# Moving the last thirteen modulation dot products of a two-layer encoder kernel to an earlier place in the program

## The chip, the cores and the metric

The kernel runs on one core of a Trainium2 chip. Its engines are TensorE (PE, whose weight loads are listed as PEld), VectorE (DVE), ScalarE (ACT), GpSimd (POOL) and SyncE (SP), whose queue issues the DMA transfers. The metric is the device time of one execution in microseconds; a kernel's time is the median of several runs.

## The reference

The reference is a trunk of two layers over one sequence of 1024 tokens with 1024 features. Layer 0 mixes tokens by differential attention (eight heads, each with two softmax maps of 64 features, whose difference weighs 128 value features), layer 1 by multi-head latent attention. Each layer first normalises its input and applies a shift and a scale that depend on a conditioning vector `c`, and at its end adds its output times a gate that depends on `c` too:

```
def _modulation(c, ada_w, ada_b):
    mod = jax.nn.silu(c) @ ada_w + ada_b
    shift, scale, gate = jnp.split(mod[:, None, :], 3, axis=-1)
    return shift, scale, gate

for i in range(DEPTH):
    shift, scale, gate = _modulation(c, ada_w[i], ada_b[i])
    h = _rmsnorm(x, norm_g[i]) * (1.0 + scale) + shift
    y = _diff_attention(h, ...) if i % N_MIXERS == 0 else _mla(h, ...)
    x = x + gate * y
return _rmsnorm(x, final_norm_g)
```

In the differential attention, `q`, `k`, `v` and a gate `z` come from one projection of `h`; queries and keys are rotated by position (rope); `p = softmax(map 0) - lam * softmax(map 1)`; the output is `p @ v`, normalised per head, times `silu(z)`, and projected by `w_out`.

## The kernel before, in words

**Precision and tiles.** A product of two float32 matrices is computed as three matmuls of rounded halves (`mm3`, high by high, high by low, low by high; lines 203 to 205). A strip is a 128-column piece of a projection for all 1024 tokens, in two halves of 512 tokens; a half takes eight steps of three matmuls. A value tile is 128 tokens by the 512 value columns of four heads, again eight steps, 24 matmuls (`v0_tile`). Value tiles are written to DRAM and read back later head by head.

**The place of the change.** The values of heads 0 to 3 are done. Then come, for head 0, the second half of the key strip, the second half of the query strip, and the gate strip (`stream0.step(Z_PRE)`, sixteen steps, both halves). After them the eight value tiles of heads 4 to 7 are computed, `tt` from 0 to 7. Ahead of tile 6 (`V_LATE`) the PSUM banks are handed out anew and the first query tile of the attention is emitted: its scores (L905), row maxima `nm` (L433), exponentials `e` (L436) and their combination (L911 to L913). The stream of strips goes on with the key strip of head 1 (`acc` with the matmuls L203 to L205).

**An eviction of a value tile** (`store_v`) is a cast on ScalarE and a subtraction on VectorE, both at L393, into a buffer `v_hl`, and a store of 512 KB into `vS` on the SP queue (L395). Tiles 0 to 5 share two buffers in the pool `p1b`, tiles 6 and 7 take theirs from the pool `pm` under the name of the dots' buffers. There are five accumulator banks up to tile 5, and two after it.

**The modulation.** `gen_mods` yields 24 dot products of 128 x 1024: sixteen for the shifts and scales of layer 1, eight for the gate of layer 0. Each one is a load of a 512 KB piece of the weights (L455, SP queue, name `ada`), and a multiply-and-sum on VectorE with a read of its accumulator (L476). Their results are needed only later: the gate column is written out (L492) for the end of layer 0, and layer 1 comes after that. Seven dots are emitted before the place of the change, two in the key half and two in the query half; from the latter's end on, their buffers are three in the pool `pm`:

```
    mod_home[0] = lambda src: mod_load(src, pm, 3)
```

The other thirteen are emitted in the loop over the value tiles, `MODS[tt]` ahead of tile `tt`.

**What sets the order.** The text gives what is emitted; a scheduler with its own costs then orders the instructions of each engine by their dependencies, so that order on an engine is not the order of the text. `tc.issue_after` and `tc.keep_in_program_order` constrain it. The rope of the first key and query strips is queued in `side` as small steps; `pend` holds those that are left, and the first four are emitted before the gate strip, two more ahead of each tile from tile 2 on. On POOL stand the rope's multiplications and subtractions (L355, L370, L377, L378) and the low halves of the strip weights (L254). The transfers L384 swap the two halves of the partitions of `qa` and `qb`. The loads L931 are weights for the query strip of head 1, issued after tile 5 (`HOLD`).

Of the kernel before, what the change touches and what calls it, by code (L numbers as in the profile page):

```python
# [44 lines left out]
SPL1 = 2  # L45
Z_PRE = 16
V_LATE = 6
MODS = (2, 2, 2, 2, 3, 2, 0, 0)
QA_V = 16
V_IN = 4  # L50
V1_AT = ((2, 4), (3, 4), (0, 6), (0, 6))
# [47 lines left out]
def trunk(ctx: ExitStack, tc: tile.TileContext, A, out):  # L99
# [186 lines left out]
    def gen_strips(items, w=None):  # L286


        w = w or split_strip(items[0][0]())
        raws = items[1][0]()  # L290
        for i, (_, rhs, consume) in enumerate(items):
            nxt = ([], [])
            at = [0, 5][: len(raws)]
            for half in range(2):
                for k, _ in enumerate(gen_half(w, rhs, half, lambda acc, half=half, consume=consume: consume(acc, half))):
                    if half == 1 and k in at:
                        for a, b in zip(nxt, split_raw(*raws.pop(0))):
                            a += b
                        if not raws and i + 2 < len(items):
                            raws = items[i + 2][0]()  # L300
                            at = at[: at.index(k) + 1]
                    yield
            w = nxt
# [191 lines left out]
    def gen_mods(load, c2):  # L495

        g, bsh, bsc, a_, b_ = mods[1]
        for j in range(KT):
            for i, (bias, acc) in enumerate(((bsh, b_), (bsc, a_))):
                mod_dot(load(A["ada_ss1"][j, i]), bias[:, j : j + 1], acc[:, j : j + 1], c2)  # L500
                if j == KT - 1 and i == 1:
                    V.scalar_tensor_tensor(out=a_, in0=a_, scalar=1.0, in1=g, op0=ALU.add, op1=ALU.mult)
                yield
        yield from gen_gate(0, load, c2)
# [178 lines left out]
    mods_g = gen_mods(lambda src: mod_home[0](src), c2)  # L683
# [192 lines left out]
    stream0 = Stream(gen_strips(items[2:], wz0))  # L876
# [13 lines left out]
    for t in pend[:4]:  # L890
        t()
    turn = 0
    stream0.step(Z_PRE)

    def q_tile(h, half, ti, zz, ep, mid=lambda i: None):

        ql = slice(ti * P, (ti + 1) * P)
        zs = [zz[:, ti : ti + 1], sm.tile([P, 1], F32, name="z1")]
        es = []
        qa, qb = QS[h][half]  # L900
        for c in range(2):
            s_ps = bank("sc", "s", [P, T])
            for src, fst in ((qa, True), (qb, False)):
                for kc in range(2):
                    PE.matmul(s_ps[:, kc * HF : (kc + 1) * HF], src[:, c, ql], KS[h][kc][:, c, :], start=fst, stop=not fst)  # L905
            with tc.issue_after(combined[-1]) if c == 0 and combined else nullcontext():
                es.append(softmax_part(None if c else ep, s_ps, zs[c], 1 if ep is a0a else 3))
            mid(c)
        e0, e1 = es
        z0, z1 = zs  # L910
        V.reciprocal(z1, z1)  # L911
        V.tensor_scalar(z1, z1, z0, neglam[:, 0:1], op0=ALU.mult, op1=ALU.mult)
        combined.append(V.scalar_tensor_tensor(out=e0, in0=e1, scalar=z1[:, 0:1], in1=e0, op0=ALU.mult, op1=ALU.add).ins)  # L913
        return e0

    first, combined = [], []
    for tt in range(8):
        if tt == V_LATE:
            psum("ps2", sc=2, tr=1, pv=1)
            zz0 = sm.tile([P, 4], F32, name="zz")  # L920
            first += [zz0, q_tile(0, 0, 0, zz0, a0a)]
        for _ in range(MODS[tt]):
            next(mods_g)
# [1220 lines left out]
```

## Time and profile before

| | us |
|---|---|
| median of three runs | 1419.05 |
| the three runs | 1411.88, 1419.73, 1419.05 |
| the profiled execution, its time | 1413.83 |
| its span | 1412.0 |
| TensorE busy in it | 1374.9 |
| VectorE busy | 936.7 |
| ScalarE busy | 740.3 |
| GpSimd busy | 610.6 |

The mean granted clock of TensorE is 0.995 of full speed. In the rows of single instructions the columns are the start in us from the span's start, the duration in us, the engine, the line of the kernel, the operation, output <- inputs, and in brackets the idle time of the engine before it with what ended it. Rows of groups have a count, then the busy time and the mean of one in ns, then the idle time before. Busy times of engines overlap; only TensorE's are near to the span.

### The profile page before, as it was taken

Reading aid. Unit: us, or ns where it says so; the run is one execution under the profiler, and the core shown is the slowest. Engines: PE = TensorE matmul, PEld = TensorE weight load, DVE = VectorE, ACT = ScalarE, POOL = GpSimd, SP = SyncE. Lnnn points to the kernel's source line nnn. Section 1 sums busy time; section 2 is a strip of 40 time slices with the busy share of each in tenths; the row PEclk is TensorE's granted clock in tenths of the full one; section 3 lists DMA queues with packets and bytes.
Section 4 is the critical chain, followed back from the end, with each engine's and each line's share of the span. In section 5 each row is a group of like instructions: output and inputs, shape, how many; then the busy total and the mean of one; then the engine's idle time right before and its main releaser. Section 6 shows DMA issues by size and latency. Waiting matters only on the chain.

```text
span 1412.0 us, 20440 instructions
## 1 busy us (share of the span) xinstructions
PE 1374.9 (97%) x7254; PEld 1150.0 (81%) x7254; DVE 936.7 (66%) x1365; ACT 740.3 (52%) x1290; POOL 610.6 (43%) x484
## 2 busy tenths in 40 slices
PE   9999899999999999999999999999999999998997
PEld 7778688888888888787778878888888888887886
DVE  7756687676777767678445787346777776764455
ACT  6623366666565655566443654345555555644342
POOL 4415164646564646462563235513142432313662
PEclk9999999999999999999999999999999999999999
DMA  9877723233333232336672222448688787776663
GB/s 352 262 226 233 237 66 103 79 103 83 105 85 95 80 96 81 97 87 221 219 240 97 97 90 90 126 146 261 164 223 248 213 240 195 204 214 214 226 213 129
DMA packets 147736, 230.98 MB, mean 164 GB/s; under 512 B 19121, under 2 KB 70449, under 8 KB 147634
## 3 DMA queue, kind: packets, MB, share of 16 engines
q1 hardware_dynamic: 147634, 229.68, 53.5%
q8 instruction: 57, 0.93, 0.3%
q14 instruction: 45, 0.37, 0.1%
HBM read 145.79 MB, written 60.23 MB: 146 GB/s over the span
## 4 chain that ended last, share of the span: by engine, by line
PE 78%; DMA 7%; DVE 6%; issue 3%; ACT 3%; SPq 2%; POOL 1%; ACTq 0%; POOLq 0%; DVEq 0%
PE acc L203 9%; PE acc L205 9%; PE acc L204 9%; PE s L1831 8%; PE s L905 7%; PE tr L414 6%; PE pv L204 4%; PE pv L205 4%; PE pv L203 4%; PE oacc L204 3%; PE oacc L205 3%; PE oacc L203 3%; PE zacc L203 1%; PE zacc L205 1%; PE zacc L204 1%
## 5 line engine op out<-in xcount | busy, mean ns | idle before, releaser
L433 DVE TENSOR_REDUCE nm<-s 128x1 f32<-128x1024 f32 x192 | 234.0, 1219 | 87.8 <-PE s L905 66.6
L416 ACT CAST pth<-tr 128x512 fp32r<-128x512 f32 x200 | 117.4, 587 | 212.8 <-PE tr L414 211.9
L436 ACT ACTIVATE e<-s,nm 128x1024 f32<-128x1024 f32 x128 | 143.2, 1119 | 94.6 <-DVE nm L433 94.2
L419 DVE TENSOR_TENSOR ptl<-tr,pth 128x512 fp32r<-128x512 f32 x200 | 137.2, 686 | 75.8 <-ACT pth L416 75.7
L254 POOL TENSOR_TENSOR wl<-wraw,wh 128x512 fp32r<-128x512 f32 (+2 forms) x82 | 102.7, 1254 | 170.4 <-ACT wh L253 162.8
L203 PE MATMUL acc<-h0h,wh 128*128 128x512 f32 x360 | 151.6, 421 | 1.8 <-DVE v_hl L393 1.7
L203 PE MATMUL pv<-pth,vt 128*128 128x256 f32 x512 | 146.4, 286 | 0.0
L204 PE MATMUL pv<-ptl,vt 128*128 128x256 f32 x512 | 145.2, 284 | 0.1
L205 PE MATMUL pv<-pth,vt 128*128 128x256 f32 x512 | 144.5, 282 | 0.0
L205 PE MATMUL acc<-h0h,wl 128*128 128x512 f32 x360 | 143.3, 398 | 0.1
L204 PE MATMUL acc<-h0l,wh 128*128 128x512 f32 x360 | 142.4, 396 | 0.0
L414 PE MATMUL tr<-ident,e 128*128 128x128 f32 x800 | 120.9, 273 | 10.1 <-DVE ptl L419 10.0
L414 PEld LDWEIGHTS tr<-ident,e 128*128 128x128 f32 x800 | 96.2, 140 | 41.6 <-DVE ptl L419 16.3
L1234 POOL TENSOR_TENSOR wol<-wor,woh 128x512 fp32r<-128x512 f32 x64 | 86.6, 1372 | 77.4 <-ACT woh L1233 71.4
L204 PEld LDWEIGHTS pv<-ptl,vt 128*128 128x128 f32 x512 | 97.2, 190 | 5.1 <-DVE ptl L419 0.4
L203 PEld LDWEIGHTS pv<-pth,vt 128*128 128x128 f32 x512 | 97.0, 189 | 4.5 <-ACT pth L416 0.4
L205 PEld LDWEIGHTS pv<-pth,vt 128*128 128x128 f32 x512 | 97.6, 191 | 0.1
L905 PE MATMUL s<-ks,qa 128*128 128x512 f32 x256 | 82.7, 403 | 6.0 <-ACT e L436 3.0
L913 DVE SCALAR_TENSOR_TENSOR e<-s,z,e 128x1024 f32<-128x1024 f32 x64 | 82.1, 1283 | 2.1
L355 POOL TENSOR_TENSOR rp_sw<-rp_sw,sinT 128x512 f32<-128x512 f32 x42 | 55.3, 1316 | 62.8 <-DMA rp_sw<-rp_raw 57.6
L205 PEld LDWEIGHTS acc<-h0h,wl 128*128 128x128 f32 x360 | 68.3, 190 | 16.4 <-POOL wl L254 0.6
L905 PE MATMUL s<-ks,qb 128*128 128x512 f32 x256 | 81.1, 396 | 0.0
(632 smaller groups left out, 3442.2 us busy)
## 6 DMA issues: line engine op xcount, KB each, us to landing
ada<-in_ada_ss SPq DMA_DIRECT2D x32, 512.0 KB, 6.4
wraw<-in_w_s SPq DMA_DIRECT2D x64, 256.0 KB, 2.8
vS<-v_hl SPq DMA_DIRECT2D x32, 512.0 KB, 5.0
vt<-vS SPq DMA_DIRECT2D x32, 512.0 KB, 5.0
wor<-in_w_out SPq DMA_DIRECT2D x64, 256.0 KB, 4.2
pS<-eT SPq DMA_DIRECT2D x28, 512.0 KB, 2.9
pr<-pS SPq DMA_DIRECT2D x56, 256.0 KB, 6.2
rp_sw<-rp_raw SPq DMA_DIRECT2D x168, 64.0 KB, 2.0
```

Of the source, the lines that this page charges most:

```text
L203: pin(PE.matmul(psum, ah, bh, start=first, stop=False))
L204: pin(PE.matmul(psum, ah, bl, start=False, stop=False))
L205: mm = PE.matmul(psum, al, bh, start=False, stop=last)
L254: sub = (lo_on or (V if pair_of else G)).tensor_sub(l_[:, :n], raw[:, :n], f32v(h_[:, :n]))
L414: pin(PE.transpose(tr[:, j, :], p[:, kt * P : (kt + 1) * P], ident))
L416: cp = S.copy(pth[kh][:, :, dst], tr)
L419: mk["V"] = V.tensor_sub(ptl[kh][:, :, dst], tr, f32v(pth[kh][:, :, dst])).ins
L433: mk["V"] = V.reduce_max(nm, s_ps, axis=AX.X, negate=True).ins
L436: ex = S.activation(e, s_ps, AF.Exp, bias=nm, scale=1.0, accum_out=zs)
L905: PE.matmul(s_ps[:, kc * HF : (kc + 1) * HF], src[:, c, ql], KS[h][kc][:, c, :], start=fst, stop=not fst)
L1234: in_turn(G.tensor_sub(lo, raw, f32v(hi)))
L1831: pin(PE.matmul(s_ps[:, kc * HF : (kc + 1) * HF], lhs, rhs(kc), start=i == 0, stop=i == 4))
```

## The change

Before, the thirteen dots are emitted 2, 2, 2, 2, 3, 2 ahead of value tiles 0 to 5. After it, three are emitted ahead of the first gate strip, two between its halves, and two ahead of each of tiles 0 to 3.

```diff
 V_LATE = 6
-MODS = (2, 2, 2, 2, 3, 2, 0, 0)
+MODS = (2, 2, 2, 2, 0, 0, 0, 0)
+MODS_Z = (3, 2)
 ...
     turn = 0
-    stream0.step(Z_PRE)
+    for n in MODS_Z:
+        for _ in range(n):
+            next(mods_g)
+        stream0.step(Z_PRE // len(MODS_Z))
```

Lines behind the second place move by up to four, lines before it by one. Computation, buffers and transfers are otherwise the same.

The first place is VectorE up to the eviction of value tile 3. Before, the last rows of that stretch read as follows; `v_hl_1291` is the eviction of tile 2, `v_hl_1338` that of tile 3, and each `ada` row is a dot, with the read of its accumulator under it.

```order
L476 ISA ada_1176,moda1_92<-ada_1176,c2_228,vec_88 128x1024
L476 ISA moda1_92 128x1
L476 ISA ada_1179,modb1_93<-ada_1179,c2_228,vec_88 128x1024
L476 ISA modb1_93 128x1
L393 TENSOR_TENSOR v_hl_1291<-vps_1266,v_hl_1291 128x512
L476 ISA ada_1211,moda1_92<-ada_1211,c2_228,vec_88 128x1024
L476 ISA moda1_92 128x1
L476 ISA ada_1214,modb1_93<-ada_1214,c2_228,vec_88 128x1024
L476 ISA modb1_93 128x1
L393 TENSOR_TENSOR v_hl_1338<-vps_1313,v_hl_1338 128x512
```

These four are dots 12 to 15 of the 24. In the changed kernel the same stretch reads so; `v_hl_1306` is tile 2 and `v_hl_1354` tile 3, and the dots of `ada_1104`, `ada_1107`, `ada_1110`, `ada_1146` and `ada_1149` (12 to 16) stand above the rows shown.

```order
L477 ISA ada_1193,gcol_1192<-ada_1193,c2_228,vec_88 128x1024
L477 ISA gcol_1192 128x1
L477 ISA ada_1196,gcol_1192<-ada_1196,c2_228,vec_88 128x1024
L477 ISA gcol_1192 128x1
L394 TENSOR_TENSOR v_hl_1306<-vps_1281,v_hl_1306 128x512
L477 ISA ada_1228,gcol_1192<-ada_1228,c2_228,vec_88 128x1024
L477 ISA gcol_1192 128x1
L477 ISA ada_1231,gcol_1192<-ada_1231,c2_228,vec_88 128x1024
L477 ISA gcol_1192 128x1
L394 TENSOR_TENSOR v_hl_1354<-vps_1329,v_hl_1354 128x512
```

Nine dots, 12 to 20, stand ahead of the eviction of tile 3, where there were four. Of the remaining four, two come before the evictions of tiles 6 and 4, in this order, and two before those of tiles 7 and 5; the first row maximum follows behind them, with no dot after it.

The second place is the SP queue, from the first dot load there. Before, `v_hl_1207` is the store of tile 0 and `v_hl_1242` that of tile 1:

```order
L230 DMA wraw_1104<-in_w_s0 128x512
L230 DMA wraw_1106<-in_w_s0 128x512
L455 DMA ada_1176<-in_ada_ss1 128x1024
L455 DMA ada_1179<-in_ada_ss1 128x1024
L395 DMA vS0_1_70<-v_hl_1207 256x4x128
L455 DMA ada_1211<-in_ada_ss1 128x1024
L455 DMA ada_1214<-in_ada_ss1 128x1024
L395 DMA vS0_1_70<-v_hl_1242 256x4x128
```

In the changed kernel `v_hl_1224` is the store of tile 0 and `v_hl_1259` that of tile 1:

```order
L456 DMA ada_1107<-in_ada_ss1 128x1024
L456 DMA ada_1110<-in_ada_ss1 128x1024
L231 DMA wraw_1113<-in_w_s0 128x512
L231 DMA wraw_1115<-in_w_s0 128x512
L456 DMA ada_1146<-in_ada_ss1 128x1024
L456 DMA ada_1149<-in_ada_ss1 128x1024
L456 DMA ada_1193<-in_ada_g0 128x1024
L456 DMA ada_1196<-in_ada_g0 128x1024
L396 DMA vS0_1_70<-v_hl_1224 256x4x128
L456 DMA ada_1228<-in_ada_g0 128x1024
L456 DMA ada_1231<-in_ada_g0 128x1024
L396 DMA vS0_1_70<-v_hl_1259 256x4x128
```

The store of tile 1 stands behind the loads of nine dots (12 to 20, that of `ada_1104` just above the rows shown) where it stood behind four. With three buffers, the load of a dot waits for the dot three before it. The cast of tile 3 on ScalarE waits for the store of tile 1, since both use the same of the two buffers.

The third place is TensorE behind the value tiles. Before, the end of value tile 7 (`vps_1473`), the third score tile and the beginning of the key strip of head 1 (`acc_1517`):

```order
L203 MATMUL vps_1473<-wvh_943,h0h7_1_132 128x512
L204 MATMUL vps_1473<-wvl_944,h0h7_1_132 128x512
L205 MATMUL vps_1473<-wvh_943,h0l7_1_133 128x512
L905 MATMUL s_1508<-ks_1091,qa_1255 128x512
L905 MATMUL s_1508<-ks_1098,qa_1255 128x512
L905 MATMUL s_1508<-ks_1091,qb_1256 128x512
L905 MATMUL s_1508<-ks_1098,qb_1256 128x512
L203 MATMUL acc_1517<-h0h0_0_102,wh_1141 128x512
```

After the change, the first score tile (`s_1424`) stands inside the strip:

```order
L206 MATMUL acc_1517<-h0h3_0_114,wl_1158 128x512
L204 MATMUL acc_1517<-h0h4_0_118,wh_1176 128x512
L205 MATMUL acc_1517<-h0l4_0_119,wh_1176 128x512
L909 MATMUL s_1424<-ks_1091,qa_1270 128x512
L909 MATMUL s_1424<-ks_1098,qa_1270 128x512
L909 MATMUL s_1424<-ks_1091,qb_1271 128x512
L909 MATMUL s_1424<-ks_1098,qb_1271 128x512
```

The first two score tiles stood within tile 7 and the third ahead of the strip; now the first two stand behind 14 matmuls of the strip. Before, tile 7 had a PSUM bank of its own beside that of tile 6, and the strip took the bank of tile 6; now tile 7 takes the bank of tile 6, and the strip the other. In both, the first matmul of tile 6 waits for the eviction of tile 3. On every engine the two orders coincide again in the attention of the first heads.

## The prediction

> **What bounds the kernel now.** I read the page first, then the stretches between 150 and 170 us, then single instructions of each engine between 120 and 163 us, because the change touches only dot products that run there.
>
> ```profile
> span 1412.0 us, 20440 instructions
> PE 1374.9 (97%) x7254; PEld 1150.0 (81%) x7254; DVE 936.7 (66%) x1365; ACT 740.3 (52%) x1290; POOL 610.6 (43%) x484
> ```
>
> TensorE is busy for 97% of the span. So whatever the change does can only be paid in TensorE idle time or in a lower granted clock, and little is left to win: 37 us in the whole span. The next view cuts out the end of the second half's value tiles. The columns are busy time of PE, PEld, DVE, ACT and POOL, the granted clock, the DMA share and GB/s.
>
> ```profile
> 150.00:155.00 5.00, 1.81 (x7) 0.86 (x5) 5.00 (x8) 1.40 (x3) 0.00 (x0) 1.00 0.91 260
> 155.00:160.00 5.00, 3.44 (x8) 2.76 (x9) 4.12 (x8) 2.18 (x4) 0.00 (x0) 0.59 0.89 288
> 160.00:165.00 5.00, 5.00 (x18) 3.91 (x18) 3.07 (x4) 0.00 (x0) 0.00 (x0) 0.73 0.65 200
> 165.00:170.00 5.00, 5.00 (x24) 3.88 (x23) 1.92 (x4) 3.26 (x6) 1.29 (x1) 1.00 0.24 59
> ```
>
> Here TensorE stands still for 4.8 us while VectorE is full, and then runs at a lowered clock. The single instructions say why: first TensorE, then VectorE and one of ScalarE.
>
> ```profile
> 121.00 0.50 PE L203 MATMUL vps<-wvh,h0h 128*128 128x512 f32 x1 [0.37 <-DVE gz L842]
> 137.49 0.39 PE L203 MATMUL vps<-wvh,h0h 128*128 128x512 f32 x1
> 153.66 0.73 PE L905 MATMUL s<-ks,qa 128*128 128x512 f32 x2 [3.04 <-ACT e L436]
> 156.56 0.80 PE L203 MATMUL acc<-h0h,wh 128*128 128x512 f32 x1 [1.72 <-DVE v_hl L393]
> 162.28 0.59 PE L204 MATMUL acc<-h0l,wh 128*128 128x512 f32 x1
> ```
>
> ```profile
> 149.94 1.28 DVE L476 CUSTOM_DVE_ANT_0 ada<-ada,c,vec 128x1024 f32<-128x1024 f32 x1
> 151.15 1.22 DVE L433 TENSOR_REDUCE nm<-s 128x1 f32<-128x1024 f32 x1
> 152.28 1.27 DVE L476 CUSTOM_DVE_ANT_0 ada<-ada,c,vec 128x1024 f32<-128x1024 f32 x1
> 153.49 1.28 DVE L476 CUSTOM_DVE_ANT_0 ada<-ada,c,vec 128x1024 f32<-128x1024 f32 x1
> 154.69 1.22 DVE L433 TENSOR_REDUCE nm<-s 128x1 f32<-128x1024 f32 x1
> 155.83 0.68 DVE L393 TENSOR_TENSOR v_hl<-vps,v_hl 128x512 fp32r<-128x512 f32 x1
> 152.40 1.11 ACT L436 ACTIVATE e<-s,nm 128x1024 f32<-128x1024 f32 x1 [3.18 <-DVE nm L433]
> ```
>
> The late dots (L476) stand between the first row maxima (nm) and the last value evictions (v_hl). The third score tile waits for the first exponential, which waited for nm behind a dot; the next strip waits for v_hl behind two dots and the second nm.
>
> I number the 24 dots in their order; the change moves 12 to 24. I number the eight value tiles of the second half of heads 0 to 7. Each tile is 24 matmuls.
>
> **Term 1, what goes: the loss around 150 to 163 us.** Idle is 3.04 + 1.72 = 4.76 us. Three tiles, 72 matmuls, lie between the starts at 121.00 and 137.49, so a step is 16.49 / 72 = 0.229 us. From 156.56 to 162.70 stand 14 matmuls, counted up to the row that follows the quoted one at 162.28; they took about 0.43 us each, 6.14 us, where 14 × 0.227 = 3.18 us were enough. The slow clock cost 2.96 us. With the dots gone from there, all of it goes: **−7.7 us**.
>
> **What the change puts in its place.** Five dots now stand before or within the first gate strip, and two before each of tiles 0 to 3. On VectorE nine dots come ahead of the eviction of tile 3, not four. This matters twice. Every dot needs a 512 KB load in one of three buffers, so the load three dots on waits for it, on the SP queue, in which the stores of finished value tiles also stand. And the dots are now where POOL is busy:
>
> ```profile
> 120.25 1.29 DVE L842 SCALAR_TENSOR_TENSOR gz<-zth,acc 128x512 f32<-128x512 f32 x2 [3.14 <-ACT zth L841]
> 122.30 0.69 DVE L359 TENSOR_TENSOR rp_r<-rp_r,rp_sw 128x512 f32<-128x512 f32 x1 [0.76 <-POOL rp_sw L355]
> 122.91 1.25 DVE L884 TENSOR_TENSOR neglam<-lp 128x1 f32<-128x1 f32 x1
> 124.27 2.33 DVE L476 CUSTOM_DVE_ANT_0 ada<-ada,c,vec 128x1024 f32<-128x1024 f32 x1
> 129.36 1.70 DVE L476 CUSTOM_DVE_ANT_0 ada<-ada,c,vec 128x1024 f32<-128x1024 f32 x1
> 138.18 1.28 DVE L476 CUSTOM_DVE_ANT_0 ada<-ada,c,vec 128x1024 f32<-128x1024 f32 x1 [1.08 <-DMA ada<-in_ada_g]
> 120.96 1.31 POOL L355 TENSOR_TENSOR rp_sw<-rp_sw,sinT 128x512 f32<-128x512 f32 x1
> 122.35 1.80 POOL L370 TENSOR_TENSOR ks<-rp_r,ks 64x512 fp32r<-64x512 f32 x1
> 125.47 2.27 POOL L377 TENSOR_TENSOR qb<-rp_r,qa 64x512 fp32r<-64x512 f32 x1
> 127.70 2.27 POOL L254 TENSOR_TENSOR wl<-wraw,wh 128x512 fp32r<-128x512 f32 x1
> 134.52 1.29 POOL L378 TENSOR_TENSOR qb<-rp_r,qa 64x512 fp32r<-64x512 f32 x1
> ```
>
> A dot alone takes 1.28 us (1.2 from the start of one to the next); next to a queue on POOL it shows 2.33, and POOL's own operations show 2.27 where one alone shows 1.29. The two take turns. Before, only four or five dots met POOL; now dots 12 to 17 do. The last rows I need are prices of transfers and of an eviction.
>
> ```profile
> vS<-v_hl SPq DMA_DIRECT2D x8, 512.0 KB, 6.3
> ada<-in_ada_g SPq DMA_DIRECT2D x8, 512.0 KB, 6.2
> ada<-in_ada_ss SPq DMA_DIRECT2D x5, 512.0 KB, 5.7
> 131.09 0.33 SPq L455 DMA_DIRECT2D ada<-in_ada_g  x1
> 134.59 0.63 SPq L395 DMA_DIRECT2D vS<-v_hl  x1
> 141.64 0.59 ACT L393 CAST v_hl<-vps 128x512 fp32r<-128x512 f32 x1 [8.44 <-DMA vS<-v_hl]
> ```
>
> The first three rows are medians from issue to landing between 110 and 165 us. Over the whole run, loads of the dots and stores of value tiles spread like this:
>
> ```profile
> DMA to landing us min/median/max: 3.8/6.4/9.9
> DMA to landing us min/median/max: 3.7/5.0/7.6
> ```
>
> **Term 2, the wait of tile 6.** Tiles 0 to 5 have two store buffers, so the cast of tile 3 waits until the store of tile 1 has landed. That store now stands in the SP queue right behind the load of dot 20, and that load waits until dot 17 has given its buffer back. Tile 6 writes the PSUM bank of tile 3. Step by step:
> - Dot 12 stands behind gz and waits for POOL's rp_sw, 120.96 + 1.31 = 122.27; it ends at 123.5.
> - neglam and rp_r (1.25 + 0.69) with one turn of POOL between: 126.6.
> - Dots 13 to 17, five turns of about 2.4: 138.7. Their loads do not set it: the load of 17 leaves after dot 14 (131.4) and lands 5.7 later, at 137.1, one turn earlier.
> - Load of dot 20 (0.33) and store of tile 1 (0.63): issued by 139.6, landed 6.3 later, 145.9.
> - Cast of tile 3 0.59, subtraction 0.69, hand-overs: tile 3 leaves its bank at 147.3.
>
> Dots 18 to 20 fit in meanwhile (load 20 lands at about 145). TensorE could have begun tile 6 at 137.5, as before: it idles **9.8 us**. With the landing at the minimum of 3.8 instead of 6.3 it is 7.3; with 9.9, the slowest of these loads, 13.4.
>
> [...]
>
> **Term 3, the clock after it.** 1.72 us of idle, a short burst of scores and 3.04 us before it lowered the clock above; one wait of 9.8 us should do it too. I take the same **2.96 us**; zero is its floor, if the wait stays short.
>
> [...]
>
> **Term 4, tile 7.** Now tile 7 takes the very bank of tile 6, so between them stand a cast and a subtraction: 0.59 + 0.69 and hand-overs, **1.6 us**. Its floor is 1.3.
>
> **Term 5, the first scores.** They have moved 14 matmuls into the key strip, and the first nm stands behind the eviction of tile 5, whose cast waits for the store of tile 3, last in a queue of loads and swaps. Work of the strip (10 matmuls, 2.3 us) lies beside it; I take **0.8 us**, between 0 and the 3.04 us that the same place shows now.
>
> Nothing else is priced: the dots, their loads and the evictions are as many as before, the two weight loads of the next key strip that are now behind three dot loads are wanted some 30 us later, and the order of the engines is the same again in the first heads' attention.
>
> Sum: 9.8 + 2.96 + 1.6 + 0.8 − 7.7 = **+7.5 us**. The profiled execution took 1413.83 us (span 1412.0), so 1421.3 on it, and 1426.6 on the median 1419.05 of the runs shown (1411.88 to 1419.73). I forecast **1424**, in the middle.
>
> **Rivals.**
> A, faster: VectorE does not wait for POOL and transfers land near their minimum. Then dot 12 ends at 122.7, dots 13 and 14 at 125.8 and 127.0, the load of 17 lands 4.2 later (0.33 + 3.8), dot 17 ends at 132.4, the store is landed at 137.1, tile 3 leaves at 138.4. Tile 6 waits 0.9 us and the clock stays up: 0.9 + 1.6 + 0.8 − 7.7 = −4.4, 1409.4 on the profiled execution and 1414.6 on the median. It decides if tile 3 is evicted by about 138. Against it: the 2.33 us of the dot beside POOL and the 6 us landings. Chance 0.12.
>
> B, hardly anything: no turns with POOL, but transfers at their medians. Dot 17 then ends with its load, 127.0 + 0.4 + 6.2, at 134.8; the store leaves at 135.8 and lands at 142.1; tile 3 is out at 143.4, the wait is 5.9: 5.9 + 2.96 + 1.6 + 0.8 − 7.7 = +3.6, so 1417.4 or 1422.6. For it: one of the dots beside POOL, at 129.36, took only 1.70. Chance 0.22.
>
> C, clearly slower: with nine 512 KB transfers closer together they land at the slow end, 9.9 us: wait 13.4, and term 5 at 3.0: 13.4 + 2.96 + 1.6 + 3.0 − 7.7 = +13.3, 1427.1 or 1432.3. For it: the DMA share of 0.91 at 150 us. Chance 0.13.
>
> D, no effect: the scheduler's order undoes the change. The instruction order shows the dots moved; 0.03.
>
> **How the numbers follow.** The forecast holds 0.5, 1421 to 1427, and its predicted time is 1424. The range goes from 1413 (below B, whose clock stretch may be missing: 1417.4 − 2.96 is about 1414) to 1431 (most of C). Left out are A on a low base and the top of C, together under 0.2. About 1%, 14 us, is what a measurement of this kernel can tell from no change. Faster by more than that would need more than the 7.7 us of term 1: 0.01. Slower by more needs C and something more: 0.05. The rest is 0.94.
>
> **What would show it.** In the changed kernel's trace: the idle rows at 153.66 and 156.56 gone and no dot left beside the first nm; dots of about 2.3 us between 121 and 138; an idle of about 10 us before a value tile's first matmul, released by v_hl, at about 137 to 147; granted clock under 1 behind it; about 1.6 us of idle one tile later. I am wrong if tile 6 begins before 141, if dots beside POOL take 1.3 us, or if a wait appears after 170 us that was not there.

## The result, and the profile after

The changed kernel takes 1419.22 us (median of 20 runs, 1414.99 to 1422.37), the kernel before, in the same comparison, 1413.28 us (20 runs, 1410.51 to 1419.73; the first three, shown above, lay on the high side). The ratio is 1.0039, 95% interval 1.0028 to 1.0049: 4.0 to 6.9 us slower, about 5.5. The profiled execution of the changed kernel took 1416.52 us.

```profile
span 1414.7 us, 20427 instructions
PE 1372.7 (97%) x7254; PEld 1149.3 (81%) x7254; DVE 937.1 (66%) x1365; ACT 741.3 (52%) x1290; POOL 608.1 (43%) x484
```

Work and busy times are what they were. The stretches of five microseconds (same columns as above: PE, PEld, DVE, ACT, POOL, granted clock, DMA share, GB/s) show a hole in TensorE at another place than before, 137 to 146 us, with the clock at 0.54 and 0.50 in the slices from 140 to 150 us:

```profile
135.00:140.00 5.00, 3.38 (x15) 2.45 (x14) 4.46 (x5) 0.03 (x1) 2.16 (x2) 1.00 0.85 283
140.00:145.00 5.00, 0.00 (x0) 0.00 (x0) 3.19 (x5) 1.03 (x2) 0.00 (x0) 0.54 1.00 320
145.00:150.00 5.00, 4.11 (x10) 3.24 (x11) 3.27 (x5) 0.11 (x1) 0.00 (x0) 0.50 1.05 308
150.00:155.00 5.00, 3.84 (x16) 2.81 (x14) 0.51 (x1) 1.07 (x2) 0.00 (x0) 0.93 0.96 288
155.00:160.00 5.00, 4.76 (x21) 3.96 (x22) 3.19 (x6) 0.00 (x0) 0.00 (x0) 1.00 0.07 18
160.00:165.00 5.00, 5.00 (x24) 4.12 (x23) 1.38 (x2) 1.18 (x2) 0.00 (x0) 1.00 1.01 280
```

The single instructions of TensorE that waited there are the first of value tile 3, of tile 6 and of tile 7. The waits of tiles 6 and 7 end with an eviction (`v_hl`); at the scores none is left.

```profile
121.72 0.50 PE L204 MATMUL vps<-wvh,h0h 128*128 128x512 f32 x1 [0.37 <-DVE gz L843]
145.89 0.79 PE L204 MATMUL vps<-wvh,h0h 128*128 128x512 f32 x1 [7.51 <-DVE v_hl L394]
155.24 0.50 PE L204 MATMUL vps<-wvh,h0h 128*128 128x512 f32 x1 [1.40 <-DVE v_hl L394]
```

The chain behind the 7.51 us is on VectorE, SP and ScalarE. The DVE rows are dots 12, 13, 14, 17 and the eviction of tile 3; the POOL rows two of GpSimd's operations beside the dots; the SP rows the loads of dots 19 and 20 and the store of tile 1; the ACT row the cast of tile 3.

```profile
122.18 1.89 DVE L477 CUSTOM_DVE_ANT_0 ada<-ada,c,vec 128x1024 f32<-128x1024 f32 x1
125.82 2.25 DVE L477 CUSTOM_DVE_ANT_0 ada<-ada,c,vec 128x1024 f32<-128x1024 f32 x1
128.01 2.30 DVE L477 CUSTOM_DVE_ANT_0 ada<-ada,c,vec 128x1024 f32<-128x1024 f32 x1
135.86 2.38 DVE L477 CUSTOM_DVE_ANT_0 ada<-ada,c,vec 128x1024 f32<-128x1024 f32 x1
145.14 0.69 DVE L394 TENSOR_TENSOR v_hl<-vps,v_hl 128x512 fp32r<-128x512 f32 x1 [0.76 <-ACT v_hl L394]
```

```profile
129.30 2.15 POOL L378 TENSOR_TENSOR qb<-rp_r,qa 64x512 fp32r<-64x512 f32 x1
131.53 2.16 POOL L379 TENSOR_TENSOR qb<-rp_r,qa 64x512 fp32r<-64x512 f32 x1
```

```profile
134.80 3.80 SPq L456 DMA_DIRECT2D ada<-in_ada_g  x2
138.70 0.64 SPq L396 DMA_DIRECT2D vS<-v_hl  x1
```

```profile
144.53 0.59 ACT L394 CAST v_hl<-vps 128x512 fp32r<-128x512 f32 x1 [3.97 <-DMA vS<-v_hl]
```

Dot 17 ends at 138.2, SP's two loads end at 138.6, the store of tile 1 leaves at 138.70, ScalarE waits for exactly this landing until 144.53, VectorE subtracts until 145.83, and tile 6 begins at 145.89. That is the chain of the prediction, link by link. As a local sum: 7.51 + 1.40 of idle, and tile 6 took 7.95 us (145.89 to 153.84) where 24 × 0.229 = 5.50 were enough, 2.45 for the clock; 11.36 us new against the 7.7 us that went, +3.6. The interval of the many runs lies a little higher, 4.0 to 6.9; experiment 6 shows why.

### The profile page after: what moved, and what is told of

Same layout as the page of the kernel before. It is cut to its first block, busy times and chain, and to the rows that moved or that the text cites. A ratio compares the mean times of both kernels' runs of the same rounds, so it can differ in the third digit from the quotient of the medians.

```text
span 1414.7 us, 20427 instructions
## 1 busy us (share of the span) xinstructions
PE 1372.7 (97%) x7254; PEld 1149.3 (81%) x7254; DVE 937.1 (66%) x1365; ACT 741.3 (52%) x1290; POOL 608.1 (43%) x484
## 4 chain that ended last, share of the span: by engine, by line
PE 76%; DVE 7%; DMA 7%; issue 3%; ACT 3%; POOL 2%; SPq 1%; DVEq 0%; ACTq 0%; POOLq 0%
PE s L1835 9%; PE acc L206 8%; PE acc L204 8%; PE acc L205 8%; PE s L909 7%; PE tr L415 5%; PE pv L205 4%; PE pv L206 4%; PE pv L204 4%; PE oacc L204 3%; PE oacc L206 3%; PE oacc L205 3%; DVE ada L477 2%; DMA ada<-in_ada_ss 1%; PE zacc L204 1%
```

## The experiments

All ratios below are to the kernel before, with the intervals of 95%; a difference in us is worked out from the ratio. "Changed" is the kernel after the change. In the first four, and in the ninth, the wait ahead of tile 6 is the number that counts.

**1. Six buffers for the dots, all else as changed.** The order of VectorE, SP and TensorE in this stretch remains the same, so only what a load waits for is different.

```diff
-    mod_home[0] = lambda src: mod_load(src, pm, 3)
+    mod_home[0] = lambda src: mod_load(src, pm, 6)
-            store_v(0, pm, acc, tt, fh, "ada", 3)
+            store_v(0, pm, acc, tt, fh, "ada", 6)
```

> The changed kernel with six instead of three buffers for the dots; the orders of VectorE, SP and TensorE in the stretch stay the same. Theory (the store of tile 1 is held in the SP queue behind the load of dot 20, which waits for dot 17): that load now waits for dot 14, over at 130.2 us, the store leaves at about 131.5 and has landed before 138; what is left is VectorE's own row of nine dots, which ends at about 142.5, so the wait ahead of value tile 6 falls from 7.5 to about 5 us and the kernel is 2 to 3 us faster than the changed kernel, still slower than before by about 3. Rival 1 (only the time of nine dots on VectorE holds the eviction of tile 3): the wait stays at 7.5 us. Rival 2 (the transfers are crowded, so earlier loads only make the stores slower): the store takes over 8 us to land and the wait stays.

Measured: 1417.07 us, ratio 1.0020 (1.0008 to 1.0032), +2.8 us. TensorE's waiting rows, then ScalarE's cast of tile 3 and VectorE's subtraction:

```profile
142.80 0.80 PE L204 MATMUL vps<-wvh,h0h 128*128 128x512 f32 x1 [4.78 <-DVE v_hl L394]
151.28 0.50 PE L204 MATMUL vps<-wvh,h0h 128*128 128x512 f32 x1 [1.40 <-DVE v_hl L394]
```

```profile
136.14 0.59 ACT L394 CAST v_hl<-vps 128x512 fp32r<-128x512 f32 x1 [6.52 <-DMA vS<-v_hl]
```

```profile
142.06 0.68 DVE L394 TENSOR_TENSOR v_hl<-vps,v_hl 128x512 fp32r<-128x512 f32 x1
```

The wait falls from 7.51 to 4.78. The store has landed at 136.14, some 8 us earlier, and the eviction now stands on VectorE directly behind dot 20, with no idle ahead of it. So the first limit is the store in the SP queue, and the row of nine dots on VectorE is the next one, which alone makes tile 6 wait 4.78 us.

**2. Without six operations of GpSimd beside the dots.** Two low halves of weights and four of queries (head 0) are copied on ScalarE instead of subtracted on GpSimd; their correction is left out.

```diff
+        if lean[1]:
+            lean[1] -= 1
+            S.copy(l_[:, :n], raw[:, :n])
+        else:
             sub = (lo_on or (V if pair_of else G)).tensor_sub(l_[:, :n], raw[:, :n], f32v(h_[:, :n]))
...
+        if lean[0]:
+            lean[0] -= 1
+            S.copy(qb[0:64, 0, :], r[0:64])
+            S.copy(qb[64:128, 1, :], r[64:128])
+        else:
             in_turn(G.tensor_sub(qb[0:64, 0, :], r[0:64], f32v(qa[0:64, 0, :])))
             in_turn(G.tensor_sub(qb[64:128, 1, :], r[64:128], f32v(qa[64:128, 1, :])))
...
+    lean[:] = 2, 2
     for n in MODS_Z:
```

> The changed kernel without six operations on GpSimd between 125 and 137 us: the low halves of the first head's queries and of two weight blocks of the next key strip are plain copies on ScalarE (the correction by the low halves is left out there). Orders of VectorE, SP and TensorE stay the same. Theory (dots and GpSimd take turns, which makes dot 17 late): dots take 1.28 us instead of about 2.3; dot 14 ends at about 128, the load of dot 17 lands at 134.3, dot 17 ends at 135.5 instead of 138.2, and the wait ahead of tile 6 falls from 7.5 to about 5 us. Rival 1 (VectorE's row of dots alone sets the eviction): nine dots at 1.2 us end before 137 and the wait falls to about 0. Rival 2 (turns do not matter, the loads' landings set everything): the wait stays at 7 to 7.5 us.

Measured: 1415.41 us, ratio 1.0011 (0.9996 to 1.0025). Tile 6's wait, then dots 13 and 17:

```profile
143.02 0.79 PE L204 MATMUL vps<-wvh,h0h 128*128 128x512 f32 x1 [5.07 <-DVE v_hl L403]
```

```profile
125.38 1.27 DVE L486 CUSTOM_DVE_ANT_0 ada<-ada,c,vec 128x1024 f32<-128x1024 f32 x1
133.40 1.28 DVE L486 CUSTOM_DVE_ANT_0 ada<-ada,c,vec 128x1024 f32<-128x1024 f32 x1 [1.60 <-DMA ada<-in_ada_g]
```

The same dots take 1.27 us where they took 2.25 to 2.38, once the six operations are off GpSimd (ScalarE makes six copies in their place), and the wait falls to 5.07. It does not fall to zero: dot 17 now waits for its load, as it had to if the loads are the next limit.

**3. Dots 12 to 24 over 8 columns.** Their loads are whole; the other 1016 columns of the sums are left out.

```diff
+        w, c_ = (w[:, :8], c_[:, :8]) if short else (w, c_)
         return V.tensor_tensor_reduce(out=w, in0=w, in1=c_, scale=0.5, scalar=bias, op0=ALU.mult, op1=ALU.add, accum_out=acc)
...
+    short.append(1)
     mod_home[0] = lambda src: mod_load(src, pm, 3)
```

> The changed kernel with dots 12 to 24 over 8 columns instead of 1024 (their loads are whole; the rest of the sum is left out). Theory: VectorE's time is gone, the chain of loads and the store stays: dot 14 ends at about 125.5, the load of dot 17 lands at 131.5, the store of tile 1 leaves at 132.5 and lands at 138.3, the eviction of tile 3 ends at 139.6; the wait ahead of tile 6 is 1.5 to 2 us and the clock stays up; the kernel is 3 to 5 us faster than before. Rival 1 (VectorE's time alone): no wait at all ahead of tile 6, 5 to 6 us faster than before. Rival 2 (transfers alone): the wait stays above 6 us and the kernel slower than before.

Measured: 1414.11 us, ratio 0.9999 (0.9987 to 1.0012), no faster than before.

```profile
140.32 0.80 PE L204 MATMUL vps<-wvh,h0h 128*128 128x512 f32 x1 [2.91 <-DVE v_hl L394]
```

Dots 17 and 18 on VectorE, what runs on GpSimd beside the first of them, and the store of tile 1:

```profile
130.67 1.33 DVE L478 CUSTOM_DVE_ANT_0 ada<-ada,c,vec 128x8 f32<-128x8 f32 x1
132.67 0.23 DVE L478 CUSTOM_DVE_ANT_0 ada<-ada,c,vec 128x8 f32<-128x8 f32 x1 [0.67 <-DMA ada<-in_ada_g]
```

```profile
129.44 2.54 POOL L255 TENSOR_TENSOR wl<-wraw,wh 128x512 fp32r<-128x512 f32 x2
```

```profile
132.45 0.64 SPq L396 DMA_DIRECT2D vS<-v_hl  x1
```

The wait is 2.91, not 1.5 to 2, and not zero: with almost no time left in the dots, the chain of loads and the store still holds the eviction too long, as the theory has it. It is not transfers alone. Dot 17 (130.67), which the load of dot 20 and so the store wait for, took 1.33 us beside an operation of GpSimd, where a dot of 8 columns takes 0.23 without one (132.67, dot 18). So some 1.1 of the 2.91 us, an estimate from these two rows, are a turn with GpSimd that a shorter dot doesn't remove, and about 1.8 are left for the transfers. The time was expected wrong, because I had the clock stay up after so short a wait. Tile 6 took 7.28 us instead of 5.50, the 1.40 us ahead of tile 7 came on top, and 2.9 + 1.8 + 1.4 = 6.1 used up what term 1 gave.

**4. No dot in the gate strip: all thirteen ahead of the first four value tiles.**

```diff
-MODS = (2, 2, 2, 2, 0, 0, 0, 0)
-MODS_Z = (3, 2)
+MODS = (4, 3, 3, 3, 0, 0, 0, 0)
+MODS_Z = (0, 0)
```

> The second part of the change alone: no dot in the gate strip, all thirteen ahead of the first four value tiles (4, 3, 3, 3). Theory: the store of tile 1 stands behind the load of dot 18, which waits for dot 15; with 2.3 us per dot from 124.3 on, dot 15 ends at 133.5, the store lands at 140.5, the wait ahead of tile 6 is about 4.3 us; with 2.4 us of slow clock, 1.4 us between tiles 6 and 7 and the 7.7 us that are saved, the kernel is about even with before (0 to +1). Rival (the five dots in the gate strip are the whole cost): no wait ahead of tile 6, 5 to 6 us faster than before.

Measured: 1415.87 us, ratio 1.0016 (1.0003 to 1.0029), +2.3 us; a little above the expected 0 to +1.

```profile
141.05 0.80 PE L204 MATMUL vps<-wvh,h0h 128*128 128x512 f32 x1 [3.74 <-DVE v_hl L394]
150.16 0.50 PE L204 MATMUL vps<-wvh,h0h 128*128 128x512 f32 x1 [0.68 <-DVE v_hl L394]
```

The wait ahead of tile 6 is there without any dot in the gate strip, 3.74 us for 4.3 expected. Dots among the first value tiles are enough to hold the store of tile 1 back; here it stands behind the load of dot 18, in the changed kernel behind that of dot 20.

**5. Five with the gate strip, the other eight where they were.**

```diff
-MODS = (2, 2, 2, 2, 0, 0, 0, 0)
+MODS = (0, 0, 1, 2, 3, 2, 0, 0)
```

> The first part of the change alone: five dots with the first gate strip (3 and 2), the other eight where they were before (ahead of value tiles 2 to 5: 1, 2, 3, 2). Theory: the store of tile 1 stands behind the load of dot 16, which waits for dot 13, over at 128 us; it has landed by 135.5, tile 3 is out by 137, tile 6 does not wait, and the late dots stand beside the first row maxima as before, with the same 4 to 5 us of idle and the slow clock: within 2 us of before. Rival (the five early dots, which meet GpSimd, are the cost): a wait of 3 us or more ahead of tile 6 and slower than before by 4 us or more.

Measured: 1414.98 us, ratio 1.0001 (0.9988 to 1.0014): even, as expected.

```profile
153.61 1.19 PE L909 MATMUL s<-ks,qa 128*128 128x512 f32 x2 [2.79 <-ACT e L437]
156.52 0.79 PE L204 MATMUL acc<-h0h,wh 128*128 128x512 f32 x1 [0.86 <-DVE v_hl L394]
```

No tile waits; the idle beside the scores is back where it was before. Neither part alone is the loss of 5.5 us: five dots in the gate strip change nothing, and thirteen among the first tiles, which put seven dots ahead of the eviction of tile 3, cost 2.3. Only the change, with five in the strip and eight among the tiles, puts nine dots ahead of that eviction and the store behind the ninth load.

**6. The kernel before, a second profile.**

> The kernel before once more, for a second profile. Theory: idle of about 4.8 us beside the first scores and a slow clock of about 6 us after it again, so that term 1 is 7.7 us in this execution too; ratio 1. Rival (the slow clock after the first scores is not there in every execution, and the gain from removing it is smaller than one profile says): full clock between 155 and 165 us, term 1 about 5 us.

Measured: 1412.22 us, ratio 0.9990 (0.9973 to 1.0006), as it must be for the same kernel. But the rival was right on term 1, which is smaller still than the 5 us that it named:

```profile
151.89 0.72 PE L905 MATMUL s<-ks,qa 128*128 128x512 f32 x2 [1.61 <-ACT e L436]
154.80 0.50 PE L203 MATMUL acc<-h0h,wh 128*128 128x512 f32 x1 [1.73 <-DVE v_hl L393]
```

```profile
155.00:160.00 5.00, 4.92 (x22) 3.77 (x21) 4.51 (x9) 0.97 (x3) 0.00 (x0) 1.00 0.75 244
160.00:165.00 5.00, 5.00 (x24) 3.97 (x24) 2.30 (x3) 2.68 (x6) 1.29 (x1) 1.00 0.72 204
```

In this execution the idle is 1.61 + 1.73 = 3.34 us and the clock is whole between 155 and 165 us. Term 1 is worth 7.7 us in one execution and 3.3 in another. By the first the change costs 11.36 − 7.7 = 3.6, by the second 8.0; the measured 4.0 to 6.9 lies between.

**7. The changed kernel, a second profile.**

> The changed kernel once more, for a second profile. Theory (the wait ahead of tile 6 comes from a chain of fixed durations): 7 to 8 us of idle there again and 1.4 us ahead of tile 7, slower than before by 4 to 7 us. Rival (the wait hangs on how transfers happen to land in one execution): it differs by more than 2 us from 7.5.

Measured: 1418.97 us, ratio 1.0036 (1.0022 to 1.0050).

```profile
143.46 0.79 PE L204 MATMUL vps<-wvh,h0h 128*128 128x512 f32 x1 [7.43 <-DVE v_hl L394]
152.83 0.50 PE L204 MATMUL vps<-wvh,h0h 128*128 128x512 f32 x1 [1.40 <-DVE v_hl L394]
```

7.43 and 1.40 for 7.51 and 1.40: what the change adds repeats itself, unlike what it removes.

**8. A third arrangement, with more buffers.** Dots 3 ahead of the gate strip and 2, 3, 3, 2 ahead of tiles 0 to 3; six buffers for the dots as in experiment 1; three store buffers.

```diff
-MODS = (2, 2, 2, 2, 0, 0, 0, 0)
-MODS_Z = (3, 2)
+MODS = (2, 3, 3, 2, 0, 0, 0, 0)
+MODS_Z = (3, 0)
...
-VB = (2, 5)
+VB = (3, 5)
```

> Thirteen dots in a third arrangement: three ahead of the gate strip, and 2, 3, 3, 2 ahead of value tiles 0 to 3, with six buffers for the dots and three store buffers for value tiles. On VectorE five dots stand ahead of the eviction of tile 3, the last ahead of the first row maximum. Theory: tile 3 is out at about 136.7, no wait ahead of tile 6 or 7 and no dot beside the scores: the whole of term 1 is saved, 5 to 8 us faster than before. Rival (thirteen loads and eight stores of 512 KB cannot pass in this time whatever their order, so some wait takes the place): a wait of 3 us or more somewhere between 135 and 160 us, within 2 us of before.

Measured: 1406.76 us, ratio 0.9943 (0.9927 to 0.9959): 8.1 us faster than before, 13.6 faster than the changed kernel. It computes everything.

```profile
140.00:145.00 5.00, 5.00 (x24) 4.15 (x23) 5.00 (x9) 1.18 (x2) 0.00 (x0) 1.00 1.06 328
145.00:150.00 5.00, 5.00 (x24) 4.09 (x23) 2.54 (x6) 0.59 (x1) 0.00 (x0) 1.00 0.59 160
150.00:155.00 5.00, 5.00 (x24) 4.11 (x23) 3.66 (x5) 2.33 (x4) 0.00 (x0) 1.00 0.69 179
```

```profile
116.25 10.35 SPq L456 DMA_DIRECT2D ada<-in_ada_g  x3
126.69 0.64 SPq L396 DMA_DIRECT2D vS<-v_hl  x1
```

TensorE has no idle of more than 0.25 us from 120 to 164 us (0.96 us follow, ahead of 165.68) and the clock is whole. The store of tile 1 leaves at 126.69, 12 us earlier than in the changed kernel, or 10 counted from the start of tile 3 in each.

**9. The same places of the dots, with the buffers as they were** (three for dots, two for stores). The edit is shown against experiment 8.

```diff
-    mod_home[0] = lambda src: mod_load(src, pm, 6)
+    mod_home[0] = lambda src: mod_load(src, pm, 3)
-VB = (3, 5)
+VB = (2, 5)
```

> The third arrangement's places of the dots (3 ahead of the gate strip; 2, 3, 3, 2 ahead of tiles 0 to 3) with the buffers as they were: three for the dots, two for stores. The store of tile 1 now stands behind the load of dot 19, which waits for dot 16. Theory (that chain sets the wait ahead of tile 6): dot 16 ends at about 135, the store leaves at 136 and lands near 142, tile 6 waits 5 to 6 us, tile 7 1.4 us: 1 to 6 us slower than before, about 10 us slower than with the buffers. Rival (the places of the dots make the third arrangement fast): no wait ahead of tile 6, 5 us or more faster than before.

Measured: 1418.88 us, ratio 1.0032 (1.0019 to 1.0045), +4.5 us.

```profile
142.89 0.79 PE L204 MATMUL vps<-wvh,h0h 128*128 128x512 f32 x1 [4.97 <-DVE v_hl L394]
165.17 0.74 PE L909 MATMUL s<-ks,qa 128*128 128x512 f32 x2 [2.17 <-ACT e L437]
```

The wait ahead of tile 6 is back, 4.97 us for 5 to 6 expected, and 2.17 us at the scores come with it. Places alone do not help.

**10 and 11. The other places with the larger buffers** (six and three): the changed kernel's, and those before the change.

> The changed kernel's places of the dots, with the six dot buffers and three store buffers of the third arrangement. On VectorE seven dots (12 to 18) stand ahead of the eviction of tile 3 instead of nine, and its cast waits for the store of tile 0 instead of tile 1. Theory (turns with GpSimd then set the end): dot 18 ends at about 139.4, tile 3 is out at 140.1, tile 6 waits 2 to 3 us, some slow clock follows, and no idle stands beside the scores: within 3 us of before, 5 us or more slower than the third arrangement. Rival (the buffers alone made the third arrangement fast, not the places of the dots): as fast as that, 6 us or more faster than before.

Measured: 1409.37 us, ratio 0.9973 (0.9963 to 0.9984), −3.8 us, a little more than the 3 us to either side that were expected; 4.3 us slower than the third arrangement, where 5 or more were expected.

```profile
137.95 0.50 PE L204 MATMUL vps<-wvh,h0h 128*128 128x512 f32 x1 [1.78 <-DVE v_hl L394]
```

> The dots where they were before the change (2, 2, 2, 2, 3, 2), with six dot buffers and three store buffers. Tiles 2 and 3 are evicted behind two dots, the first scores stand within value tile 6, and seven dots still stand behind the first row maximum. Theory: tiles 6 and 7 lie beside the first exponentials, the late dots cost VectorE time next to the scores: 1 to 5 us faster than before, 3 us or more slower than the third arrangement. Rival (buffers alone): as fast as the third arrangement, 6 us or more faster than before.

Measured: 1408.45 us, ratio 0.9968 (0.9955 to 0.9982), −4.5 us.

```profile
153.49 0.50 PE L203 MATMUL acc<-h0h,wh 128*128 128x512 f32 x1 [1.76 <-DVE v_hl L393]
168.31 0.73 PE L905 MATMUL s<-ks,qa 128*128 128x512 f32 x2 [1.32 <-ACT e L436]
```

The buffers change more than any placing: with them the same three placings go from 0, +5.5 and +4.5 us to −4.5, −3.8 and −8.1. Both kinds of buffers were raised together here. Six for the dots alone took 2.7 us off the changed kernel (experiment 1) and left it slower than before; three for the stores alone were not run, so what each kind is worth is not shown. What is left with the early placing is a wait of tile 6 for the seventh dot (1.78); with the late one, the waits beside the scores.

**12. A fourth arrangement, buffers as in 8:** all thirteen ahead of tiles 0 to 4.

```diff
+MODS = (2, 3, 3, 3, 2, 0, 0, 0)
+MODS_Z = (0, 0)
```

> All thirteen dots ahead of value tiles 0 to 4 (2, 3, 3, 3, 2), six buffers for the dots and three store buffers. On VectorE two dots stand ahead of the evictions of tiles 2 and 3, and four still beside the first row maxima, two of them between the first and the second. Theory: no wait ahead of tile 6; the scores stand within value tile 7, whose matmuls cover the first exponential, so little idle is left: 3 to 6 us faster than before, less than with no dot there. Rival (any dot beside the scores costs its whole time): 2 to 3 us of idle behind the scores and a slow clock, within 2 us of before.

Measured: 1409.21 us, ratio 0.9959 (0.9945 to 0.9973), −5.8 us, as expected; the third score tile waits 0.91 us.

## Why the prediction was right, and where its sizes were off

The sign, the rough size and the mechanism held: +5.5 us measured (4.0 to 6.9) for +7.5 forecast, 1419.22 us in the range and 5 below the 1424 forecast. Some 3 of those 5 us come from the base: the first three runs had a median of 1419.05, which became 1413.28 with more runs, and the forecast stood halfway between 1419.05 and the profiled execution. That the sum itself came within 2 us is partly luck: the four terms of new cost were 15.16 us together where 11.36 were measured, 3.8 too much, and the 7.7 us set against them were too much as well, so that the two errors offset each other. Of the signs that were named for being wrong none came: tile 6 began at 145.89, four of the dots beside GpSimd took 2.25 to 2.38 us, and from 170 to 300 us TensorE idles 0.1 to 0.3 us in each of the four profiles of the two kernels.

- **Term 1, what goes.** Its place was right; no idle is left beside the scores. Its size, 7.7, was that of one execution; a second shows 3.3 (experiment 6): the slow clock behind the idle, 3.0 us, is not always there, and the idle was 1.4 us shorter. This was the step on which a single profile could not be trusted, and I had given it no range.
- **Term 2, the wait of tile 6: 9.8 forecast, 7.51 and 7.43 measured.** Counted from the start of tile 3 (121.00 before, 121.72 after), the store left 1.0 us earlier than forecast: there was no turn of GpSimd between neglam and rp_r, dot 13 began 1.5 us sooner for it, and 0.5 of this was lost again up to SP's issue. The cast began 5.2 us after SP had issued the store, not 6.3, which is another 1.1. Of this 0.6 is a slip of the sum: the 6.3 of its row counts from the start of an issue, and the sum added it to the end of one (139.6), so the 0.63 us of issuing stand in it twice. Counted as in the row, from 138.70, the landing took 5.8. The lower bound given, 7.3, holds by a hair. Experiments 1, 2 and 3 each take one link away (the load that waits for dot 17, the turns with GpSimd, most of the time of the dots) and the wait falls to 4.78, 5.07 and 2.91; with all thirteen dots ahead of the first row maximum it goes to nothing only where buffers cut the chain and fewer dots stand ahead of the eviction (experiment 8).
- **The turns with GpSimd** are shown by experiment 2: 1.27 us a dot without them, 2.25 to 2.38 with them. In the changed kernel dots start 2.23 us apart (128.01, 130.24) and GpSimd's operations too (129.30, 131.53), one of each in turn. A dot of 8 columns, 0.23 us alone, took 1.33 us beside such an operation (experiment 3): it ended at 132.00, and GpSimd's two operations at 131.98. What makes the two engines take turns is not shown.
- **Term 3, the clock: 2.96 forecast, 2.45 and 2.47 measured.** Right in kind. The floor of zero "if the wait stays short" was too hopeful: 2.91 us of idle in experiment 3 still cost 1.8.
- **Term 4, tile 7: 1.6 forecast, 1.40 measured** in both profiles.
- **Term 5, the first scores: 0.8 forecast,** no idle row there in either profile. It was on the safe side of its bounds.
- **The rivals.** A (faster) is out: its condition, tile 3 evicted by 138, was missed by 8 us. B (no turns) is out by experiment 2: without turns the wait is 5.07, near B's 5.9, with turns 7.5. C (slow transfers) is out: the store landed in 5.8 us, counted as in the row, not in 9.9, which was the slowest time of a load; the row of the stores ended at 7.6.

## What to carry to other kernels

Moving work to an earlier place moves its loads too, and a load that waits for a buffer can hold back what stands behind it in its queue; here it was a store whose buffer a later eviction needed, which left at 138.70 us behind such a load, and at 130.42 when the loads had six buffers (experiment 1). Before moving, look at what the moved loads will wait for and which stores stand behind them; if there is room, give them more buffers first, and the stores too: here both together gained 4.5 us with the order left as it was, while no order that was run gained anything without them. And take the worth of a removed wait from two executions when a clock drop is part of it: here it was 7.7 us in one and 3.3 in the other.

## What the runs showed of the hardware that I had not expected

The stretches of half clock do not go by the length of the idle beside them: 10.24 us of half clock stand beside 7.51 of idle, 3.41 beside 4.78. From the clock record of the fourteen traces, their lengths, and those of the stretches of full clock between them, are whole multiples of 3.41 us, but for the last one, which the end of the trace cuts off. Near the place of the change:

```
kernel                       idle beside it (us)       half clock (us)
before, first profile        3.04 and 1.72             6.83
before, second profile       1.61 and 1.73             none
changed, both profiles       7.51; 7.43                10.24; 10.24
experiment 1 (six buffers)   4.78                      3.41
experiment 2 (GpSimd)        5.07                      6.83
experiment 3 (short dots)    2.91                      3.41
experiment 4                 3.74                      6.83
experiment 5                 2.79 and 0.86             6.83
experiment 9                 4.97                      6.83
experiment 10                1.78                      3.41
experiment 11                1.76                      none
experiments 8 and 12         0.96; 0.91                none
```

Beside 1.78 us of idle the clock went to half once, beside 1.76 us it did not, nor beside 3.34 us in two pieces; and 4.78 us were followed by a shorter stretch than 3.74 us. So the length of a wait does not decide alone. What else decides is not shown: the kernel before lost 3.0 us to the slow clock in one execution, with 3.04 and 1.72 us of idle, and nothing in another, with 1.61 and 1.73.

Such stretches also stand where the change has no part: one of 3.41 or 6.83 us starts between 1269 and 1285 us in twelve of the fourteen profiles, but not in the changed kernel's first profile nor in experiment 10's. A stretch of 3.41 us costs about 1.7 us where TensorE works through it, an estimate from the half clock; in experiment 3, with one such stretch, tile 6 took 1.78 us more than the 5.50 of full clock. So the times of two single executions can differ by some us without the change (the kernel before took 1410.51 to 1419.73 in 20 runs), and a local sum is to be held against many runs.
